# Gate and up projections of an FFN by Strassen's seven block products, with x and the inner chunks passing through DRAM

## The chip, the cores and the metric

The kernel runs on one core of one Trainium2 chip. The metric is device time in microseconds, the median of the runs. The core's engines are TensorE (PE, with PEld for its weight loads), VectorE (DVE), ScalarE (ACT), GpSimd (POOL) and SyncE (SP), which here issues all DMAs. Each takes its instructions in the order in which the program was laid out, and waits on semaphores for the others.

## The reference

One step of a decoder trunk with two layers, on 1024 prompt tokens and 8 sample tokens (T = 1032), model width 1024, all in float32:

```
x = x + short_conv(rmsnorm(x))            # layer 0: h @ w_in (1024 x 3072), a 3-tap convolution, @ w_out
x = x + swiglu(rmsnorm(x), w_gu[0], w_down[0])
k, v = rmsnorm(x) @ w_kv                  # one shared K/V, rotary on k
x = x + window_attention(rmsnorm(x) @ w_q, k, v) @ w_o      # layer 1: 16 heads, window 128, sinks
x = x + swiglu(rmsnorm(x), w_gu[1], w_down[1])
y = rmsnorm(x)

def swiglu(h, w_gu, w_down):
    g, u = split(h @ w_gu, 2)             # w_gu 1024 x 5632: 2816 columns of gate, 2816 of up
    return (silu(g) * u) @ w_down         # w_down 2816 x 1024
```

Outputs are y for both groups and the new convolution and K/V state.

## The kernel before, in words

Everything is kept transposed: the width lies in the 128 partitions, in NC = 8 chunks, and the tokens in the free dimension. x, Hh and Hl are tiles of 128 x 8 x 1032 that stay in SBUF. Tokens go in three tiles TT of 384, 384 and 264.

A product is made exact to float32 from operands split in a high and a low part (fp32r). `split` (L131) makes the high part on ACT and the low one, source minus high, on DVE; `load_w` (L79) fetches a weight unit of 1024 columns (512 KB) and splits it likewise, its subtraction on DVE, or on POOL where `lo=G`. `mm3` (L117) issues, for each row chunk, three matmuls on L122 to L124: high x high, high x low, low x high, all into one PSUM bank.

`ffn` (L346): for each of NJ = 22 column chunks j two units of weights are loaded (gate, up). For each token tile a gate group of 8 x 3 matmuls is made, multiplied by 1/rms (DVE) and put through Silu (ACT), an up group likewise, and their product split into a chunk of hidden operands fhh, fhl, which stays in SBUF. After 5, 5, 5, 3 and 4 chunks a round of the down projection (`down_round`, L220) takes the chunks gathered so far and adds into x, a bank at a time (`x_add`, L218, DVE). In the last round x is finished token tile by token tile: its squares are summed (ACT and POOL, L143 and L147), `prep` (L206) writes the next operands Hh and Hl, x times the norm's gain, and `stats` (L190) computes 1/rms. `stats` consists of `rms_tokens` (L158: matmuls against ones and eleven small DVE operations, L168 to L175, then three on L178) and `spread` (L183: a matmul), each traced a number of matmul groups later by `later` and `tick`.

Ahead of the first FFN stands the convolution, which ends in a second round of w_out (four hidden chunks) with `after_tile`. Ahead of the second FFN stands the attention: `attend` (L464) works off 32 blocks of 128 queries and one group of the samples, and fills PE's waits between them in small steps with the value rows and with `out_projection` (L658), which for a token tile loads w_o's eight units (low parts on POOL), multiplies, and adds to x. A tile's projection starts as the blocks of its tokens are done (`ends`), and what is left of the last one runs after them.

The order of instructions on each engine isn't that of the text. A planner goes through the program at compile time and takes, engine by engine, what is ready by its own reckoning, earlier lines first; buffers (wraw three, wh and wl four each, eight PSUM banks) hold it back. The order of DMAs on SP is planned in the same way.

Of the kernel before, what the change touches and what calls it, by code (L numbers as in the profile page):

```python
# [16 lines left out]
P = 128  # L17
# [29 lines left out]
def trunk_kernel(ctx, tc, A):  # L47
# [7 lines left out]

    x = const.tile([P, NC, T], F32, name="x")
# [22 lines left out]
    def load_w(src, n, lo=V, rows=None, raw=None, parts=1):  # L79
        """A weight unit as exact high and low parts; rows scales it by a norm's gain."""  # L80
# [18 lines left out]
    def mm_tile():  # L99
        return pools[-1].tile([P, 512], F32, name="mm")  # L100
# [48 lines left out]
    def token_blocks(ti):  # L149
        """(first token to sum, first column, columns) of a tile's blocks."""  # L150
        w = TT[ti][1] - TT[ti][0]
# [6 lines left out]
    def rms_tokens(acc, ti):  # L158
        """1/rms of a tile's tokens, with the tokens in the partitions."""
        at = token_blocks(ti)  # L160
# [4 lines left out]
        st = nt.tile([P, 2, 4], F32, name="nst", bufs=1)  # L165
        v, z = st[:, 0, :n], st[:, 1, :n]
        y = inv_tok[:, ti, :n]
# [15 lines left out]
    def spread(dg, ti):  # L183
        """The diagonals summed into every partition."""
        w = TT[ti][1] - TT[ti][0]
        ib = mm_tile()
        PE.matmul(ib[:, :w], ones, dg[:, :w], start=True, stop=True)
        return ib[:, :w]

    def stats(acc, ti, first, second, then=None):  # L190
        """inv of a tile, its two steps traced after as many matmul groups."""
        a, b = TT[ti]

        def one():
            dg = rms_tokens(acc, ti)

            def two():
                S.activation(inv[:, a:b], spread(dg, ti), AF.Copy)
# [7 lines left out]
    def prep(k, a, b, gi):  # L206
        """Operands of one chunk: x times the gain, still without 1/rms."""
# [12 lines left out]
    def down_round(hid, w_dram, nk, gi=None, after_tile=None):  # L220
        """x += W^T hid for nk chunks of hid; with after_tile, token tile by token tile,
        with the next phase's operands (gain gi) made as x is done."""
# [23 lines left out]
        for ti, (a, b) in enumerate(TT):  # L246
            acc = new_acc()
            for m in range(NC):
                part(units[m // per], m, a, b)
                sq_acc(acc, m, a, b)  # L250
                if gi != "final":
# [3 lines left out]
    def conv_mixer():  # L255
        with tc.tile_pool(name="cv", bufs=2) as cv:
# [9 lines left out]
            def gate(cv, i, ti, pcxb, ub, hh, hl):  # L266
                """One tile of the convolution's input, itself, and its gate."""
# [36 lines left out]
            for i in range(NC):  # L304
# [31 lines left out]
                if i == r1 - 1:  # L336
                    after = None
# [603 lines left out]
```

## Time and profile before

| | |
|---|---|
| median of 3 runs | 2292.16 us (2289.47 to 2292.61) |
| span of the profiled execution | 2287.1 us (its page gives no time beside the span) |
| PE busy | 2243.5 us, 98%, 14010 matmuls |
| DVE, ACT, POOL busy | 1028.1, 572.4, 325.0 us |
| DMA | 151.04 MB, mean 66 GB/s |

The span runs from the first to the last instruction. A busy share is the time in which an engine has an instruction at work; matmuls overlap one another, so that PE's busy time is not the sum of their durations. The two FFNs take about 1500 of the 2287 us.

### The profile page before, as it was taken

The page shows a single profiled execution, that of the slowest core. Times are in us where ns is not written, and L with a number is a line of the kernel's source. Part 1 is how long each engine was busy: PE and PEld are TensorE (multiplying, and loading weights), DVE is VectorE, ACT ScalarE, POOL GpSimd, SP SyncE. Part 2 cuts the span into 40 slices and gives each one's busy share as a digit, 9 for nine tenths or more (in the row PEclk, how much of TensorE's full clock was granted, in tenths as well). Part 3 has the DMA queues.
Part 4 walks back from the last instruction along what each step waited for, and adds up shares of the span by engine and source line. Part 5 has one row for each costly group of instructions (what it writes and reads, how often), then busy time and mean ns, then how long its engine had stood idle before and what let it go on. Part 6 is the DMA issues. An engine that isn't in the chain of part 4 may idle for free.

```text
span 2287.1 us, 33543 instructions
## 1 busy us (share of the span) xinstructions
PE 2243.5 (98%) x14010; PEld 2176.4 (95%) x14010; DVE 1028.1 (45%) x1834; ACT 572.4 (25%) x1119; POOL 325.0 (14%) x415
## 2 busy tenths in 40 slices
PE   8999999999999999999999999999999999999997
PEld 7999999999999999999899857889999999999997
DVE  7443447333333333343675465563333333333345
ACT  5110114221211211212332465542112111111122
POOL 4210114000000000000353444630000000000004
PEclk9999999999999999999999999999999999999999
DMA  5111111112112112111054554431111121111102
GB/s 189 50 56 37 56 49 45 34 35 71 34 41 65 35 40 62 40 56 47 25 174 141 152 135 121 130 93 46 39 56 46 39 61 41 46 53 51 47 29 75
DMA packets 87831, 151.04 MB, mean 66 GB/s; under 512 B 9920, under 2 KB 58576, under 8 KB 87520
## 3 DMA queue, kind: packets, MB, share of 16 engines
q1 hardware_dynamic: 87680, 148.90, 22.0%
q8 instruction: 110, 1.80, 0.3%
q14 instruction: 41, 0.34, 0.0%
HBM read 133.75 MB, written 17.23 MB: 66 GB/s over the span
## 4 chain that ended last, share of the span: by engine, by line
PE 90%; DVE 5%; ACT 2%; DMA 1%; issue 1%; POOL 1%; SPq 0%; DVEq 0%; ACTq 0%; POOLq 0%
PE mm L122 28%; PE mm L124 28%; PE mm L123 28%; PE po L569 2%; PE sc L535 1%; PE pt L555 1%; DVE Hl L133 1%; DVE x L218 1%; DMA x<-xT 1%; DVE Hl L213 1%; ACT sq L143 1%; POOL acc L147 0%; ACT Hh L212 0%; DVE inv_tok L175 0%; DVE wl L94 0%
## 5 line engine op out<-in xcount | busy, mean ns | idle before, releaser
L122 PE MATMUL mm<-Hh,wh 128*128 128x384 f32 (+1 forms) x3120 | 1003.2, 322 | 7.0 <-ACT wh L93 5.4
L123 PE MATMUL mm<-Hl,wh 128*128 128x384 f32 (+1 forms) x3120 | 1000.5, 321 | 3.5 <-DVE Hl L213 3.5
L124 PE MATMUL mm<-Hh,wl 128*128 128x384 f32 (+1 forms) x3120 | 999.2, 320 | 0.4 <-DVE wl L94 0.4
L122 PEld LDWEIGHTS mm<-Hh,wh 128*128 128x128 f32 x3120 | 588.2, 189 | 10.8 <-ACT wh L93 5.4
L123 PEld LDWEIGHTS mm<-Hl,wh 128*128 128x128 f32 x3120 | 588.3, 189 | 9.0 <-DVE Hl L213 7.4
L124 PEld LDWEIGHTS mm<-Hh,wl 128*128 128x128 f32 x3120 | 587.8, 188 | 1.8 <-DVE wl L94 1.0
L93 ACT ACTIVATE wh<-wraw 128x1024 fp32r<-128x1024 f32 (+3 forms) x222 | 216.0, 974 | 573.2 <-PE mm L123 568.5
L124 PE MATMUL mm<-fhh,wl 128*128 128x384 f32 (+1 forms) x1056 | 339.7, 322 | 0.0
L122 PE MATMUL mm<-fhh,wh 128*128 128x384 f32 (+1 forms) x1056 | 339.6, 322 | 0.0
L123 PE MATMUL mm<-fhl,wh 128*128 128x384 f32 (+1 forms) x1056 | 337.7, 320 | 0.0
L218 DVE TENSOR_TENSOR x<-mm,x 128x384 f32<-128x384 f32 (+1 forms) x312 | 159.7, 513 | 295.9 <-PE mm L124 295.5
L94 DVE TENSOR_TENSOR wl<-wraw,wh 128x1024 fp32r<-128x1024 f32 (+3 forms) x198 | 222.0, 1122 | 51.9 <-ACT wh L93 51.0
L367 DVE TENSOR_TENSOR fh<-mm,sg 128x384 f32<-128x384 f32 x132 | 68.1, 516 | 371.9 <-PE mm L124 371.9
L147 POOL TENSOR_TENSOR acc<-acc,sq 128x384 f32<-128x384 f32 (+1 forms) x105 | 111.3, 1060 | 810.2 <-ACT sq L143 806.5
L123 PEld LDWEIGHTS mm<-fhl,wh 128*128 128x128 f32 x1056 | 199.8, 189 | 0.4
L122 PEld LDWEIGHTS mm<-fhh,wh 128*128 128x128 f32 x1056 | 199.5, 189 | 0.4
L124 PEld LDWEIGHTS mm<-fhh,wl 128*128 128x128 f32 x1056 | 199.6, 189 | 0.0
L132 ACT ACTIVATE fhh<-fh 128x384 fp32r<-128x384 f32 x132 | 64.9, 492 | 378.9 <-DVE fh L368 377.1
L362 DVE TENSOR_TENSOR sg<-mm,inv 128x384 f32<-128x384 f32 x132 | 68.1, 516 | 179.2 <-PE mm L124 179.2
L363 ACT ACTIVATE sg<-sg 128x384 f32<-128x384 f32 x132 | 64.4, 488 | 285.0 <-DVE sg L362 285.0
L88 POOL TENSOR_TENSOR wraw<-wraw,sm 128x1024 f32<-128x1024 f32 x12 | 24.4, 2034 | 708.8 <-DMA wraw<-w_k 701.7
L133 DVE TENSOR_TENSOR fhl<-fh,fhh 128x384 fp32r<-128x384 f32 x132 | 67.9, 514 | 50.9 <-ACT fhh L132 50.9
(109 smaller groups left out, 1582.3 us busy)
## 6 DMA issues: line engine op xcount, KB each, us to landing
wraw<-w_gu SPq DMA_DIRECT2D x88, 512.0 KB, 3.6
q<-qd SPq DMA_DIRECT2D x128, 128.0 KB, 2.9
wraw<-w_down SPq DMA_DIRECT2D x48, 320.0 KB, 2.9
wraw<-w_o SPq DMA_DIRECT2D x24, 512.0 KB, 4.0
wraw<-w_in SPq DMA_DIRECT2D x23, 512.0 KB, 3.6
qd<-stg SPq DMA_DIRECT2D x8, 768.0 KB, 3.6
wraw<-w_out SPq DMA_DIRECT2D x8, 512.0 KB, 3.7
wraw<-w_down SPq DMA_DIRECT2D x8, 512.0 KB, 3.7
```

The lines of the kernel that those rows point to most:

```text
L93: S.activation(wh[:, c], raw[:, c], AF.Copy)
L94: lo.tensor_tensor(wl[:, c], raw[:, c], wh[:, c].bitcast(F32), op=ALU.subtract)
L122: PE.matmul(out, wh[:, c], xh, start=i == 0, stop=False)
L123: PE.matmul(out, wh[:, c], xl, start=False, stop=False)
L124: PE.matmul(out, wl[:, c], xh, start=False, stop=i == n - 1)
L132: S.activation(hi, src, AF.Copy)
L133: eng.tensor_tensor(lo, src, hi.bitcast(F32), op=ALU.subtract)
L147: G.tensor_tensor(acc[:, :w], acc[:, :w], sq[:, :w], op=ALU.add)
L218: V.tensor_tensor(x[:, m, a:b], ps, x[:, m, a:b], op=ALU.add)
L362: V.tensor_tensor(sg[:, :w], pg[:, :w], inv[:, a:b], op=ALU.mult)
L363: S.activation(sg[:, :w], sg[:, :w], AF.Silu)
L367: V.tensor_tensor(h[:, :w], pu[:, :w], sg[:, :w], op=ALU.mult)
```

## The change

Gate and up are no longer computed chunk by chunk but as a 2 x 2 block product: the width in two halves (row chunks 0 to 3 and 4 to 7), the tokens in two halves of 516 (each in two tiles of 258, FT), the output columns in pairs of chunks m and m + 11. Of the eight products of blocks seven remain, by the form of Strassen's method with 15 additions. A unit n is one such pair, of the gate (n even) or the up projection (n odd), 22 units a layer. Four additions are made on the weights (POOL, in `pair_units`), four on x (`ffn_operands`, DVE and POOL, in place), and seven on the results, of which those into one bank are made by PE, which goes on adding into it after ACT has copied its state out.

The operands are now x times gain and 1/rms, so that the factor 1/rms is no longer applied to the results. x itself is written to DRAM (xd) before it is scaled and read back before the down projection; its place in SBUF holds Strassen's differences, then temporaries of the gate and up units. The hidden chunks go to DRAM (hd) and come back, in the order HID, into Hh and Hl, four chunks at a time, for a down projection that now follows all units, in rounds of 4, 4, 4, 4, 2 and 4. The second w_out round and out_projection go by the four tiles FT; the last out_projection is left over and run inside `ffn`.

```diff
+TH = T // 2
+TS = TH // 2
+FT = [(i * TS, (i + 1) * TS) for i in range(4)]
+NP = NJ // 2
+HID = [c for m in range(NP) for c in (m, m + NP)]
-FFN_ROUNDS = [(0, 5), (5, 10), (10, 15), (15, 18), (18, 22)]
+FFN_ROUNDS = [(0, 4), (4, 8), (8, 12), (12, 16), (16, 18), (18, 22)]
...
+    xd = dr.tile([P, NC, T], F32, name="xd")
+    hd = dr.tile([NJ, P, 2, T], F32, name="hd")
...
+    k0, k1 = slice(0, 4), slice(4, 8)
+    def extra_splits(s):
+        a0, b0 = FT[s]
+        a1, b1 = FT[2 + s]
+        for e, src in enumerate((x[:, k1, a1:b1], x[:, k0, a1:b1], x[:, k1, a0:b0])):
+            split(extra["h"][:, e, :, a0:b0], extra["l"][:, e, :, a0:b0], src)
+
+    def ffn_operands(ti):
+        s = ti % 2
+        a0, b0 = FT[s]
+        a1, b1 = FT[2 + s]
+        if ti < 2:
+            for k in (k0, k1):
+                split(Hh[:, k, a0:b0], Hl[:, k, a0:b0], x[:, k, a0:b0])
+            return
+        b11, b12, b21, b22 = (x[:, k, c] for k in (k0, k1) for c in (slice(a0, b0), slice(a1, b1)))
+        split(Hh[:, k1, a1:b1], Hl[:, k1, a1:b1], b22)
+        V.tensor_tensor(b11, b12, b11, op=ALU.subtract)
+        split(Hh[:, k0, a1:b1], Hl[:, k0, a1:b1], b11)
+        G.tensor_tensor(b12, b22, b12, op=ALU.subtract)
+        V.tensor_tensor(b22, b22, b11, op=ALU.subtract)
+        G.tensor_tensor(b21, b21, b22, op=ALU.subtract)
+        if extra:
+            extra_splits(s)
+        else:
+            owed.append(s)
+
+    def ffn_tile(acc, ti, gi, first, second):
+        a, b = FT[ti]
+        Q.dma_start(xd[:, :, a:b], x[:, :, a:b])
+        def one():
+            dg = rms_tokens(acc, b - a, None)
+            def two():
+                iv = spread(dg, b - a)
+                for k in range(NC):
+                    V.scalar_tensor_tensor(
+                        x[:, k, a:b], x[:, k, a:b], gain(gi, k), iv, op0=ALU.mult, op1=ALU.mult
+                    )
+                ffn_operands(ti)
+            later(second - first, two)
+        later(first, one)
...
-        for ti, (a, b) in enumerate(TT):
+        for ti in (0, 2, 1, 3) if tiles is FT else range(len(tiles)):
+            a, b = tiles[ti]
...
+                        tiles = FT
+                        after = lambda acc, ti: ffn_tile(acc, ti, 1, 2, 5)
...
+    def pair_units(w_dram, own):
+        def load(n):
+            w = w_dram[:, n * 2048 : (n + 1) * 2048]
+            r1, r2 = fetch(w[:, 0:1024], 1024), fetch(w[:, 1024:2048], 1024)
...
+            G.tensor_tensor(s1, a21, a22, op=ALU.add)
+            parts(a11)
+            G.tensor_tensor(a21, a11, a21, op=ALU.subtract)
+            parts(s1)
+            G.tensor_tensor(a11, s1, a11, op=ALU.subtract)
+            parts(a11)
+            G.tensor_tensor(s4, a12, a11, op=ALU.subtract)
+            parts(s4)
+            parts(a21)
+            parts(a12)
+            parts(a22)
+            return dict(zip((1, 5, 6, 3, 7, 2, 4), out))
...
+        def group(ps, w, p, s, first):
+            wh, wl = w[p]
+            for k in range(4):
+                xh, xl = operand(p, k, s)
+                c = slice(k * P, (k + 1) * P)
+                for i, (lhs, rhs) in enumerate(((wh, xh), (wh, xl), (wl, xh))):
+                    PE.matmul(
+                        ps[:, s, :TS], lhs[:, c], rhs, start=first and k == 0 and i == 0,
+                        stop=k == 3 and i == 2, skip_group_check=not first,
+                    )
+            tick()
+
+        def finish(m, q, s):
+            S.activation(hi[q][:, s].bitcast(F32R), hv[q][:, s], AF.Copy)
+            V.tensor_tensor(
+                hv[q][:, s].bitcast(F32R), hv[q][:, s], hi[q][:, s], op=ALU.subtract
+            )
+            if s.stop == 2:
...
+                Q.dma_start(
+                    hd[2 * m + (q > 20), :, :, c],
+                    x[:, k, :].rearrange("p (h c) -> p h c", h=2),
+                )
...
+        def up_step(p, banks, s, m):
+            X, Y, Z = (b[:, s, :TS] for b in banks)
+            if p == 1:
+                S.activation(p1[:, s], X, AF.Copy)
+            elif p == 5:
+                S.activation(p5[:, s], Y, AF.Copy)
+            elif p == 6:
+                S.activation(u2[:, s], X, AF.Copy)
+            elif p == 3:
+                V.tensor_tensor(hv[12][:, s], Y, u2[:, s], op=ALU.add)
+                V.tensor_tensor(hv[12][:, s], hv[12][:, s], sg[12][:, s], op=ALU.mult)
+                finish(m, 12, s)
+            elif p == 7:
+                S.activation(u3[:, s], X, AF.Copy)
+                G.tensor_tensor(hv[22][:, s], u3[:, s], p5[:, s], op=ALU.add)
+                G.tensor_tensor(hv[22][:, s], hv[22][:, s], sg[22][:, s], op=ALU.mult)
+                finish(m, 22, s)
+            elif p == 2:
+                V.tensor_tensor(hv[11][:, s], Z, p1[:, s], op=ALU.add)
+                V.tensor_tensor(hv[11][:, s], hv[11][:, s], sg[11][:, s], op=ALU.mult)
+                finish(m, 11, s)
+            else:
+                V.tensor_tensor(hv[21][:, s], X, sg[21][:, s], op=ALU.mult)
+                finish(m, 21, s)
+
+        bank = {1: 0, 6: 0, 7: 0, 4: 0, 5: 1, 3: 1, 2: 2}
+        for n in range(2 * NP):
+            m, step = n // 2, up_step if n % 2 else gate_step
+            w = load(n)
+            banks = [pools[-1][0].tile([P, 2, 512], F32, name="mm2") for _ in range(3)]
+            for subs in ((0,), (1,)) if n == 0 else ((0, 1),):
+                for p in (1, 2, 5, 3, 6, 7, 4) if n == 0 else (1, 5, 6, 3, 7, 2, 4):
+                    for s in subs:
+                        group(banks[bank[p]], w, p, s, p in (1, 2, 5))
...
+    def ffn(layer, gi, after, lead=None):
...
+            for n in "hl":
+                extra[n] = ff.tile([P, 3, 4, TH], F32R, name=f"ex{n}")
+            while owed:
+                extra_splits(owed.pop(0))
...
+            if lead is not None:
+                lead()
+            gate_up(layer, ff)
...
+        for k in range(NC):
+            Q.dma_start(x[:, k], xd[:, k])
...
+            for r, (r0, r1) in enumerate(FFN_ROUNDS):
+                last = r == len(FFN_ROUNDS) - 1
+                hid = []
+                for j in range(r0, r1):
+                    if last:
+                        h = fd.tile([P, T], F32R, name=f"hh{j - r0}")
+                        l = fd.tile([P, T], F32R, name=f"hl{j - r0}")
+                    else:
+                        k = 4 * (r % 2) + j - r0
+                        h, l = Hh[:, k], Hl[:, k]
+                    Q.dma_start(h.bitcast(F32), hd[j, :, 0])
+                    Q.dma_start(l.bitcast(F32), hd[j, :, 1])
+                    hid.append((h, l))
+                down_round(hid, A[f"w_down{layer}_{r}"], r1 - r0, gi, after if last else None)
...
+        work = [Block(g, i) for i in range(SEQ // W) for g in range(NKV)]
+        work.insert(26, Samples())
+        ends = [12, 20, 29, len(work)]
```

`gate_step` does for the gate what `up_step` does for the up projection: four copies and four Silu on ACT, two additions on DVE, one on POOL. In the first w_out tiles' order (0, 2, 1, 3) tiles 0 and 2 belong to the first half product of unit 0, tiles 1 and 3 to the second. `hi` and `hv` lie in x's chunks 0 to 3, the gate's results in chunks 4 and 5, weight sums in chunks 6 and 7. For products 1 and 5 the operands are Hh's and Hl's chunks 0 to 3, for 2 and 3 chunks 4 to 7, for 6, 7 and 4 the extra splits.

## Rows read from the trace of the kernel before

**Rows 1.** Page: busy us by engine; granted clock, tenths in 40 slices.

```profile
PE 2243.5 (98%) x14010; PEld 2176.4 (95%) x14010; DVE 1028.1 (45%) x1834; ACT 572.4 (25%) x1119; POOL 325.0 (14%) x415
...
PEclk9999999999999999999999999999999999999999
```

**Rows 2.** Page, the chain that ended last: share by engine and line.

```profile
PE 90%; DVE 5%; ACT 2%; DMA 1%; issue 1%; POOL 1%; SPq 0%; DVEq 0%; ACTq 0%; POOLq 0%
PE mm L122 28%; PE mm L124 28%; PE mm L123 28%; PE po L569 2%; PE sc L535 1%; PE pt L555 1%; DVE Hl L133 1%; DVE x L218 1%; DMA x<-xT 1%; DVE Hl L213 1%; ACT sq L143 1%; POOL acc L147 0%; ACT Hh L212 0%; DVE inv_tok L175 0%; DVE wl L94 0%
```

**Rows 3.** Windows: stretch, length, busy us PE PEld DVE ACT POOL, clock, DMA.

```profile
341.00:390.00 49.00, 45.64 (x290) 44.63 (x288) 36.22 (x75) 24.14 (x48) 19.30 (x19) 1.00 0.12 36
390.00:1080.00 690.00, 689.97 (x4379) 689.64 (x4380) 260.08 (x441) 130.77 (x206) 4.22 (x4) 1.00 0.17 48
...
1266.00:1480.00 214.00, 207.74 (x1130) 154.94 (x1129) 126.87 (x230) 123.07 (x379) 108.08 (x198) 0.98 0.51 138
1480.00:1525.00 45.00, 40.70 (x277) 36.83 (x276) 31.09 (x49) 24.91 (x41) 25.89 (x17) 1.00 0.40 117
```

**Rows 4.** Timeline, PE: start, busy us, line, operation; stretches of 48, 96, 33.

```profile
646.46 0.28 PE L122 MATMUL mm<-Hh,wh 128*128 128x264 f32 x1
...
652.27 0.34 PE L122 MATMUL mm<-Hh,wh 128*128 128x384 f32 x1
...
669.09 0.28 PE L122 MATMUL mm<-Hh,wh 128*128 128x264 f32 x1
...
1268.07 0.28 PE L478 MATMUL mm<-wl,Hh 128*128 128x256 f32 x1
...
1271.99 0.28 PE L478 MATMUL mm<-wl,Hh 128*128 128x256 f32 x1
```

**Rows 5.** Lines by form: shapes, count | busy us, mean ns | idle before.

```profile
L94 DVE TENSOR_TENSOR wl<-wraw,wh 128x1024 fp32r<-128x1024 f32 x138 | 171.4, 1242 | 42.1 <-ACT wh L93 41.2 <-POOL acc L147 0.6
...
L218 DVE TENSOR_TENSOR x<-mm,x 128x384 f32<-128x384 f32 x208 | 115.4, 555 | 210.3 <-PE mm L124 209.9
...
L94 POOL TENSOR_TENSOR wl<-wraw,wh 128x1024 fp32r<-128x1024 f32 x24 | 57.8, 2413 | 17.8 <-ACT wh L93 17.6
...
L218 DVE TENSOR_TENSOR x<-mm,x 128x264 f32<-128x264 f32 x104 | 44.4, 430 | 85.6 <-PE mm L124 85.5
...
L147 POOL TENSOR_TENSOR acc<-acc,sq 128x264 f32<-128x264 f32 x35 | 36.0, 1030 | 33.6 <-ACT sq L143 32.7
...
L557 DVE TENSOR_TENSOR pc<-pt,cst 128x512 f32<-128x512 f32 x32 | 22.0, 687 | 13.9 <-PE pt L555 13.9
...
L544 ACT ACTIVATE comb<-sc 128x512 f32<-128x512 f32 x32 | 19.1, 596 | 17.8 <-PE sc L535 16.9 <-POOL comb L499 0.6
...
L784 DVE SCALAR_TENSOR_TENSOR x<-x,sm,mm 128x264 f32<-128x264 f32 x6 | 2.5, 481 | 1.8 <-ACT inv L773 1.8
```

**Rows 6.** Timeline, ACT, in the first FFN.

```profile
604.18 1.06 ACT L93 ACTIVATE wh<-wraw 128x1024 fp32r<-128x1024 f32 x1 [1.01 <-PE mm L123]
605.14 0.41 ACT L363 ACTIVATE sg<-sg 128x264 f32<-128x264 f32 x1
```

**Rows 7.** Timeline, DVE and POOL, 1497 to 1507 us.

```profile
1499.97 2.31 DVE L173 TENSOR_TENSOR nst<-inv_tok 128x3 f32<-128x3 f32 x1
...
1505.35 0.16 DVE L173 TENSOR_TENSOR nst<-inv_tok 128x3 f32<-128x3 f32 x1
...
1506.53 0.68 DVE L178 TENSOR_SCALAR dg<-cst,inv_tok 128x128 f32<-128x128 f32 x3
...
1497.53 4.74 POOL L94 TENSOR_TENSOR wl<-wraw,wh 128x1024 fp32r<-128x1024 f32 x2
```

**Rows 8.** Windows at 10 us; DMA issues, us to landing; timeline of SP.

```profile
10.00:20.00 10.00, 8.00 (x38) 6.42 (x38) 10.00 (x10) 7.46 (x15) 6.97 (x6) 1.00 1.06 381
...
qd<-stg SPq DMA_DIRECT2D x4, 528.0 KB, 4.0
...
19.37 0.63 SPq L792 DMA_DIRECT2D o_ks<-cache_k  x1
```

More of the change, by code (lines that the diff above doesn't have):

```diff
@@ L250, in down_round @@
                 sq_acc(acc, m, a, b)
-                if gi != "final":
+                if gi not in ("ffn", "final"):
                     prep(m, a, b, gi)
@@ new lines, in out_projection, with attention @@
+    def out_projection(ti):
+        a, b = FT[ti]
+        w = b - a
+        acc = new_acc()
+        xs = h_chunks(a, b)
+        for m in range(NC):
+            u = load_w(A["w_o"][:, m * 1024 : (m + 1) * 1024], 1024, lo=G)
+            ps = mm_tile()
+            for part in (range(0, 4), range(4, 8)):
+                mm3(ps[:, :w], *u, 0, xs, part)
+                yield
+            x_add(ps[:, :w], m, a, b)
+            sq_acc(acc, m, a, b)
+        ffn_tile(acc, ti, 4, 2, 4)
+    def attention(psum):
@@ L722, in attend @@
                 ti += 1
-        for _ in fill:
-            pass
+        return fill
     def start():
@@ new lines, in final, with one, two, scale @@
+    def final(acc, ti):
+        a, b = TT[ti]
+        last = b == T
+        def one():
+            dg = rms_tokens(acc, b - a, inv_tok[:, ti])
+            if last:
+                while pending:
+                    pending.pop(0)[1]()
+            later(0 if last else 2 + ti, partial(two, dg))
+        def two(dg):
+            iv = spread(dg, b - a)
+            S.activation(inv[:, a:b], iv, AF.Copy)
+            for n in range(4):
+                later(0 if last else n + ti, partial(scale, iv, 2 * n))
+        def scale(iv, k0):
+            for k in (k0, k0 + 1):
+                y = x[:, k, a:b]
+                if k in ((1, 4, 7), (), (4, 5))[ti]:
+                    G.tensor_tensor(y, y, inv[:, a:b], op=ALU.mult)
+                    S.activation(y, y, AF.Copy, scale=gain(5, k))
+                else:
+                    V.scalar_tensor_tensor(
+                        y, y, gain(5, k), iv, op0=ALU.mult, op1=ALU.mult
+                    )
+            Q.dma_start(A["o_y"][:, k0 : k0 + 2, a:b], x[:, k0 : k0 + 2, a:b])
+        later(0 if last else 2, one)
@@ new lines, in finish_tile @@
+    def finish_tile(rest):
+        for _ in rest:
+            pass
+    with tc.tile_pool(name="ps1", bufs=8, space=bass.MemoryType.PSUM) as psp:
+        pools.append((psp, False))
+        conv_mixer()
+        pools.pop()
+    psum = ffn(0, None, lambda acc, ti: stats(acc, ti, 2, 4 if ti == 2 else 8))
+    rest = attention(psum)
+    psum = ffn(1, "final", final, partial(finish_tile, rest))
+    psum.close()
+    Q.dma_start(A["o_ks"], A["cache_k"])
+    Q.dma_start(A["o_vs"], A["cache_v"])
@@ L800, in _units, with _quarters @@
         w[(k0 + k) * P : (k0 + k + 1) * P, c] for c in cols for k in range(nk)
+    ]
+def _quarters(w, pairs):
+    return [
+        w[(4 * h + k) * P : (4 * h + k + 1) * P, _chunk_cols(m)]
+        for pair in pairs for h in range(2) for m in pair for k in range(4)
     ]
```

250 lines of the change are left out of this document (127 added, 123 removed).

## The prediction

> **What bounds the kernel now.** Read in this order. First the page's busy shares [rows 1]: TensorE (PE) is busy 98% of the span, DVE 45%, ACT 25%, POOL 14%, and the reader should see nines in the granted clock from end to end. Then the chain that ended last [rows 2]: 90% of it is PE, 28% on each of the three lines of mm3. Then the stretches [rows 3]: in the first FFN (the second is alike) PE is busy 689.97 of 690 us, while DVE has 260. Nothing there waits, so a matmul taken out of an FFN is time taken out. PE stands still only where phases meet: 3.4 us of 341 to 390 (conv to FFN) and 4.3 us of 1480 to 1525 (attention to FFN). What a matmul costs isn't its busy time (they overlap) but the distance between starts [rows 4]: 48 starts with 264 columns take 652.27 - 646.46 = 5.81 us, 121.0 ns each; the next 96 with 384 columns take 16.82 us, 175.2 ns each; 33 with 256 columns take 3.92 us, 118.8 ns each.
>
> **Gate and up, what goes and what comes.** Before, a layer has 44 column chunks x 8 row chunks x 3 matmuls = 1056 per token tile; over two layers 4224 wide ones and 2112 of 264 columns: 4224 x 0.1752 + 2112 x 0.1210 = 995.6 us. After, a layer has 22 units x 7 products x 4 row chunks x 3 x 2 half tiles = 3696 of 258 columns, 7392 in all: fewer columns by 1/8, but more instructions. No row has 258 columns. From below 258/384 of 175.2 ns = 117.7 ns, from above a line through the rows with 256 and 264 columns, 119.4. I take 119 ns, since the 256 row is nearest: 879.6 us (870.1 to 882.6). Taken away: 116.0 us (113.0 to 125.5).
>
> Tiles of 258 also come into the second w_out round (4 x 96 x 0.119 = 45.7 us for 45.3) and into w_o (+0.9): together +1.3. The down projection keeps its columns. Its sixth round adds 24 x_add a layer, beside PE: a round of two chunks has 8 x 6 x (2 x 0.1752 + 0.1210) = 22.6 us of PE and 16 x 0.555 + 8 x 0.430 = 12.3 us of DVE adds [rows 5].
>
> **Inside the loop of units.** One unit is 168 x 0.119 = 20.0 us of PE, a product 2.86 us. The helpers, by [rows 5], with 512 columns on ACT at 0.60, DVE at 0.69, POOL at 1.3 (between 1.03 at 264 columns and 2.41 at 1024): seven weight splits and eight evacuations on ACT, 7 x 0.6 + 8 x 0.6 = 9.0 us; on DVE in an up unit seven weight subtractions and nine operations on the results, 16 x 0.69 = 11.0 us; on POOL four weight sums and, in an up unit, two operations more, 7.8 us. All fit in 20. Products 1, 6, 7, 4 grow in one bank, and each must be read by ACT (0.6 us) before the next is added; another product of 2.86 us lies between, so the reading is covered 4 times over. The same cover stands for the last product, which the next unit's second one waits for. Weight parts are made while the unit before runs: the order on an engine isn't the order of the text, since [rows 6] ACT makes the next chunk's wh at 604.18, ahead of the Silu of the present one. I take 3 us for both layers (0 to 25).
>
> A rule speaks against this loop. In the trace, DVE's L173 on three elements takes 2.31 us while a POOL subtraction of 2.4 us runs, and 0.16 us without one; it ends as POOL's ends [rows 7]. The Trainium skill (SBUF — State Buffer, "SBUF: two separate sides") says the same: a DVE operation with two SBUF inputs and a POOL operation share a pair of ports as an exclusive lock, and the later one blocks. In an up unit two-input work of DVE is 13 x 0.69 = 9.0 us, so by the rule the pair is held 9.0 + 7.8 = 16.8 of 20.0 us: tight, but not the bound, and this term stays.
>
> **Conv to FFN, the dear place.** Count from the start of the second w_out round; a tile is 96 x 0.119 = 11.4 us, the round ends at 45.7. All of the following falls on DVE [rows 5, 7], and SBUF-only work of 1032 columns is taken at 1.25 from the 1024 row. Statistics 11 operations 0.2 apart and 0.68: 2.9. Scaling x, eight at 0.48: 3.9. Operands: tiles 0 and 1 two subtractions, 2.5; tiles 2 and 3 four operations, 5.0, and three extra splits, 3.75. From 14.3 us, when tile 0's sum is there, until product 5 of the second half can start: tile 0 9.3, tile 2 11.8, tile 1 9.3, tile 3 as far as its difference's low part 10.6, 22 x_add 9.5, unit 0's weights 4.8, the first half's extra splits 3.75: 59 us, so 73.3 at the earliest. PE wants that product after 45.7 + 9 half products of 1.43 = 58.6. A gap of 15 us. POOL holds 16 us of additions, 9.6 of differences and 5 of weight sums in that time; if a tenth of it blocks DVE, 3 us more (0 to 19, its share beside two-input work). Less the 3.4 us that PE loses there now [rows 3]: +15 (8 to 31).
>
> **Attention to FFN.** The last w_o tile (22.8 us) runs after the blocks, so tile 2's operands have cover. Tile 3's chain of 10.6 can't start before 22.8 + 2.9 (two groups of unit 0), so it ends at 36.3, where PE wants product 5 at 22.8 + 9 x 1.43 = 35.7. Tile 2's 15.5, x_add's 3.4 and the weights' 4.8 lie before it on DVE, 27 us from about 3 us on. POOL has w_o's low parts at 2.4 each, four differences and the weight sums; half of these last 14.6 us held against DVE makes 7. Gap about 8, less 4.3 of now: +4 (0 to 25). In attention itself eight more w_o units cost POOL 19 us of 214, where it is busy 108 [rows 3]: hidden but for +2 (0 to 10).
>
> **Gate and up to down.** x and four hidden chunks come back from DRAM. The chunks are 8 loads of 528 KB, 4.3 MB; at the 381 GB/s that 10 to 20 us shows 11.3 us, and 4.0 us for the first [rows 8]. Hh's first half is free after product 5 of the last unit, 5 x 2.86 = 14.3 us before the end, so these loads are covered. x's first chunk waits for the stores of product 2 (0.69 x 3 + 0.6 + 4.0 = 6.7 us after it) and queues behind the second round's eight loads: it lands some 11 us after the end. x_add is then late, but eight banks hold eight tiles, 15 us of PE. That holds if SP lets a ready load pass a waiting one. It does so where the planner saw it so: o_ks, last in the text, is issued at 19.37 [rows 8]. I take 2.5 us at each of two places (0 to 22). Over the down rounds 22 x 1.06 MB + 11.5 MB in 249 us is 139 GB/s, far below 381.
>
> **The sum.** 2287.1 - 116.0 + 1.3 + 3 + 15 + 4 + 2 + 5 = 2201.4 us of span. The page's execution gives its span alone; the median of the runs, 2292.16, lies 5.1 above it. Forecast 2206.5 us.
>
> **Rivals.**
> - The meeting points cost no more than now, because the planner lets other work into DVE's waits: 2287.1 - 114.7 + 5.1 + some 4 = 2182 us. For it: DVE is at 74% in 341 to 390 [rows 3] and PE lost only 3.4 us. Against: the sum of 59 us on one engine. 20%.
> - Loads in the wrong order and POOL's holds in full. If x's loads stand ahead of the chunks on SP, the first group of each down phase waits about 6.7 + 11.3 + 4.0 = 22 us, twice, where I have 5; with POOL's holds in full at conv to FFN 16 more: 2206.5 + 39 + 16 = 2261.5 us, half of it 2234. For it: x's loads come first in the text. 12%.
> - Slower than before: late reading in the bank that four products share. ACT and DVE take work in order, and DVE can hang behind POOL. If every reading there ends later than 2.86 us after its product, PE waits at 4 x 44 = 176 places. It decides from (2292.2 - 2206.5)/176 = 0.49 us of lateness on; at 1 us the time is 2206.5 + 176 = 2382.5. For it: DVE's waits for POOL [rows 7], and that ACT's copies stand behind copies that wait for DVE. Against: four-fold cover and ACT at half load. That the change doesn't save matmul time because a weight load bounds 258 columns is excluded by the 118.8 ns at 256 columns. 6%.
>
> **Chances.** Forecast (2192 to 2230) 60%, the rivals 20, 12 and 6; 2% within 0.2% of now, which is about what a measurement of this kernel can tell from no change. So faster 0.92, same 0.02, slower 0.06. The range reaches from the first rival to the dear case, 2178 to 2255, and leaves out some 15%.
>
> **What would show it.** Starts of 258-column matmuls 118 to 119.5 ns apart, 168 of them in about 20 us; no PE wait inside units. In the round before the first FFN, DVE busy without a break and PE idle some 15 us ahead of the second half of unit 0. At both starts of the down phase, PE idle below 5 us and the chunks' loads issued before those of x's first chunks. It would be wrong if units last more than 20.7 us (a wait a product), or if the meeting points cost over 70 us together.

## The result, and the profile after

The changed kernel takes 2251.99 us (median of 4 runs, 2251.54 to 2253.41) against 2291.85 for the kernel before beside it: ratio 0.9828 [0.9814, 0.9842]. The forecast was 2206.5. The gain is there, 39.9 us, but less than half of the 85.7 forecast. The profiled execution has a span of 2251.6 us, 35.5 less than before.

The page's busy shares and clock, which answer to [rows 1], and its chain by engine and line [rows 2]:

```profile
PE 2166.4 (96%) x15370; PEld 2093.3 (93%) x15370; DVE 1127.8 (50%) x1896; ACT 743.5 (33%) x1421; POOL 697.6 (31%) x689
...
PEclk9999999999999999999999999898999999999998
...
PE 87%; DVE 6%; POOL 2%; ACT 2%; issue 2%; DMA 1%; SPq 0%; DVEq 0%; POOLq 0%; ACTq 0%
PE mm L500 38%; PE mm L135 14%; PE mm L136 14%; PE mm L137 14%; PE po L838 2%; DVE Hl L146 1%; PE sc L804 1%; POOL acc L160 1%; PE pt L824 1%; DMA x<-xT 1%; DVE x L229 1%; ACT Hh L145 1%; PE mm L176 0%; POOL wl L103 0%; ACT sq L156 0%
```

POOL's work has doubled, the clock row has lost its unbroken nines, and PE has given 3% of the chain to the helpers. Where that is, the windows say (columns as in [rows 3]):

```profile
341.00:390.00 49.00, 39.55 (x313) 39.01 (x312) 34.53 (x78) 15.40 (x31) 27.57 (x28) 0.92 0.23 66
390.00:440.00 50.00, 38.63 (x251) 36.04 (x251) 42.71 (x75) 24.76 (x43) 19.14 (x15) 0.87 0.15 44
440.00:860.00 420.00, 420.00 (x3499) 420.00 (x3498) 183.18 (x257) 177.82 (x310) 151.99 (x112) 1.00 0.36 117
1400.00:1470.00 70.00, 62.83 (x357) 47.67 (x357) 42.00 (x82) 35.48 (x92) 43.63 (x50) 0.87 0.51 142
1470.00:1520.00 50.00, 39.20 (x304) 36.31 (x302) 30.44 (x48) 20.10 (x29) 35.81 (x21) 0.91 0.37 105
1520.00:1570.00 50.00, 40.72 (x274) 38.77 (x275) 36.12 (x52) 22.92 (x42) 25.16 (x17) 0.84 0.23 74
1565.00:1985.00 420.00, 417.14 (x3473) 416.94 (x3472) 187.76 (x261) 177.68 (x309) 151.56 (x112) 1.00 0.36 117
```

The reader is to see two things. Between 440 and 860 us the loop of units keeps PE busy 420.00 of 420 us, with every helper below half load. Around it PE is idle 21 of 99 us at conv to FFN and 27 of 170 at attention to FFN, where before it was idle 3.4 and 4.3 (in 49 and 45 us). The waits of PE in these two stretches (engine and line that waited, what for: us in total, times, longest), 340 to 440 first:

```profile
PE mm L176 <- POOL acc L160: 13.8, 3, 8.1
PE mm L500 <- DVE Hl L146: 3.0, 1, 3.0
```

and 1480 to 1600:

```profile
PE mm L500 <- DVE wl L146: 12.0, 1, 12.0
PE mm L500 <- ACT wh L145: 3.0, 1, 3.0
PE mm L500 <- DVE Hl L146: 2.6, 1, 2.6
```

For a ledger, read the starts of PE's matmuls: from the start of the second w_out round to the first scores of the attention ("first place": conv to FFN, first FFN, rotary) and from there to the last matmul ("second place": attention, its end, second FFN). Before they last 940.9 and 999.6 us, after 914.4 and 992.2. With 258-column matmuls at the 120.1 ns that the loop shows, matmuls alone would make them 887.8 and 947.4. So the first place costs 26.6 us more than before and the second 44.8, beside what the matmuls save. Together with 105.3 us saved on matmuls and 1.6 ahead of the first place: -105.3 + 26.6 + 44.8 - 1.6 = -35.5, the change of the span.

### The profile page after: what moved, and what is told of

It is laid out like the page before. It is cut to its first block, busy times and chain, and to the rows that moved or that the text cites. A ratio compares the mean times of both kernels' runs of the same rounds, so it can differ in the third digit from the quotient of the medians.

```text
span 2251.6 us, 37629 instructions
## 1 busy us (share of the span) xinstructions
PE 2166.4 (96%) x15370; PEld 2093.3 (93%) x15370; DVE 1127.8 (50%) x1896; ACT 743.5 (33%) x1421; POOL 697.6 (31%) x689
## 4 chain that ended last, share of the span: by engine, by line
PE 87%; DVE 6%; POOL 2%; ACT 2%; issue 2%; DMA 1%; SPq 0%; DVEq 0%; POOLq 0%; ACTq 0%
PE mm L500 38%; PE mm L135 14%; PE mm L136 14%; PE mm L137 14%; PE po L838 2%; DVE Hl L146 1%; PE sc L804 1%; POOL acc L160 1%; PE pt L824 1%; DMA x<-xT 1%; DVE x L229 1%; ACT Hh L145 1%; PE mm L176 0%; POOL wl L103 0%; ACT sq L156 0%
## 5 line engine op out<-in xcount | busy, mean ns | idle before, releaser
L135 PE MATMUL mm<-Hh,wh 128*128 128x384 f32 (+2 forms) x1936 | 614.7, 318 | 8.3 <-ACT wh L102 5.4
L136 PE MATMUL mm<-Hl,wh 128*128 128x384 f32 (+2 forms) x1936 | 613.4, 317 | 2.8 <-DVE Hl L224 2.8
L137 PE MATMUL mm<-Hh,wl 128*128 128x384 f32 (+2 forms) x1936 | 611.5, 316 | 2.7 <-POOL wl L103 2.6
L500 PE MATMUL mm<-Hh,wl 128*128 128x258 f32 x1408 | 400.6, 285 | 12.0 <-DVE wl L146 12.0
L500 PE MATMUL mm<-Hl,wh 128*128 128x258 f32 x1408 | 401.5, 285 | 5.6 <-DVE Hl L146 5.6
L500 PE MATMUL mm<-Hh,wh 128*128 128x258 f32 x1408 | 402.8, 286 | 4.0 <-ACT wh L145 3.0
L500 PE MATMUL mm<-exh,wh 128*128 128x258 f32 x1056 | 299.0, 283 | 2.3 <-ACT u L532 2.0
L500 PE MATMUL mm<-exl,wh 128*128 128x258 f32 x1056 | 298.8, 283 | 1.2 <-DVE exl L146 1.2
L500 PE MATMUL mm<-exh,wl 128*128 128x258 f32 x1056 | 299.4, 284 | 0.0
L500 PEld LDWEIGHTS mm<-Hh,wl 128*128 128x128 f32 x1408 | 269.2, 191 | 12.4 <-DVE wl L146 12.4
L500 PEld LDWEIGHTS mm<-exh,wh 128*128 128x128 f32 x1056 | 200.2, 190 | 3.6 <-ACT u L532 2.8
```

Of the source, the lines that this page charges most:

```text
L135: PE.matmul(out, wh[:, c], xh, start=i == 0, stop=False)
L136: PE.matmul(out, wh[:, c], xl, start=False, stop=False)
L137: PE.matmul(out, wl[:, c], xh, start=False, stop=i == n - 1)
L500: PE.matmul(ps[:, s, :TS], lhs[:, c], rhs, start=first and k == 0 and i == 0, stop=k == 3 and i == 2, skip_group_check=not first,)
```

## The experiments

Each is the changed kernel with the edit shown, unless it says otherwise. "Places" are the added costs by that ledger, from each profiled execution. Where nothing was edited in it, the first moves by some 2 us (26.4 to 28.3 in e2, e12, e15 and e16), but the second by 8: e3, whose edit lies in the first place, has 36.6 there. Differences of that size aren't read; where the 8 us come from is shown under "The clock". The changed kernel was not run again beside the edits, so two runs are taken as different where the intervals of their ratios are apart.

| run | us, median | ratio to before | places |
|---|---|---|---|
| changed kernel | 2251.99 | 0.9828 [0.9814, 0.9842] | 26.6, 44.8 |
| e1_ops_dve | 2242.62 | 0.9774 [0.9759, 0.9790] | 23.1, 41.1 |
| e2_wo_dve | 2252.32 | 0.9823 [0.9806, 0.9839] | 26.5, 42.9 |
| e3_stats_late | 2251.21 | 0.9821 [0.9799, 0.9843] | 29.4, 36.6 |
| e4_tiles258 | 2308.60 | 1.0066 [1.0053, 1.0079] | |
| e6_defer | 2246.45 | 0.9798 [0.9777, 0.9819] | 23.2, 37.8 |
| e7_no_extras | 2265.94 | 0.9886 [0.9870, 0.9901] | 37.0, 45.9 |
| e8_bare | 2242.77 | 0.9784 [0.9771, 0.9797] | 23.8, 35.5 |
| e10_defer_both | 2238.42 | 0.9758 [0.9743, 0.9774] | 21.6, 34.2 |
| e11_bare_k1 | 2218.31 | 0.9678 [0.9665, 0.9692] | 9.4, 28.1 |
| e12_keep_warm | 2249.53 | 0.9814 [0.9799, 0.9828] | 28.3, 39.0 |
| e13_best | 2233.56 | 0.9750 [0.9736, 0.9765] | 21.4, 31.1 |
| e14_defer_ops | 2242.79 | 0.9788 [0.9775, 0.9801] | 23.3, 34.8 |
| e15_late | 2247.69 | 0.9812 [0.9798, 0.9825] | 26.6, 39.0 |
| e16_wo_all | 2250.12 | 0.9821 [0.9808, 0.9835] | 26.4, 40.8 |
| e17_best2 | 2238.53 | 0.9771 [0.9754, 0.9788] | 21.8, 30.7 |
| e18_best3 | 2233.91 | 0.9750 [0.9737, 0.9764] | 20.6, 31.2 |

The first theories, on what holds PE up where phases meet (the "meeting points"): A, POOL is late there and the other queues stand behind it; B, DVE has too much to do; C, PE's own order puts a waiting instruction ahead of ready ones.

**The price of the matmul.** The kernel before, with gate and up in four tiles of 258 tokens and no Strassen:

```diff
-                for a, b in TT:
+                for a, b in [(i * 258, (i + 1) * 258) for i in range(4)]:
```

> The kernel before with gate and up groups in four token tiles of 258 in place of 384, 384 and 264, no block products: the price of the narrower matmul by itself. At the 119 ns of the forecast two layers gain 2 x 1056 x (4 x 119 - 471.4 ns) = 9.7 us, 2302 us; at the 120.1 ns that lie between starts in the changed kernel 19 us, 2311 us. If narrow tiles bring waits of their own (evacuations, weights), more than 2316.

It took 16.6 us more than the kernel before. 8448 such matmuls replace 995.6 us, so one costs (995.6 + 16.6)/8448 = 119.8 ns. In the changed kernel itself, two starts, the second 51 matmuls after the first (timeline of PE, columns as in [rows 4]):

```profile
599.77 0.28 PE L500 MATMUL mm<-exh,wh 128*128 128x258 f32 x1
...
605.89 0.28 PE L500 MATMUL mm<-Hh,wh 128*128 128x258 f32 x1
```

That is 120.0 ns each.

**POOL's differences moved to DVE** (e1):

```diff
-        G.tensor_tensor(b12, b22, b12, op=ALU.subtract)
+        V.tensor_tensor(b12, b22, b12, op=ALU.subtract)
...
-        G.tensor_tensor(b21, b21, b22, op=ALU.subtract)
+        V.tensor_tensor(b21, b21, b22, op=ALU.subtract)
```

> The changed kernel with the two subtractions of ffn_operands that were on POOL (1032 columns, 2.4 us each) made on DVE. Theory A, POOL is late where phases meet and PE waits in order behind it: the 8.1 us for which PE waits for POOL's sum of squares in the second w_out round go to under 3, time 2240 to 2246 us. Theory B, the amount of DVE work at the meeting points is what lasts: DVE gets 2.5 us more a tile, time 2254 to 2262. Theory C, PE's own order is at fault, the statistics' matmul standing ahead of groups that don't need it: the wait stays above 6 us, time 2250 to 2254.

9.4 us came back, as A expected; PE's longest wait for the sums fell from 8.1 to 5.0 us, not under 3. The timeline of the changed kernel at conv to FFN, DVE and then POOL, shows why taking work onto the busier engine helps:

```profile
376.17 5.02 DVE L146 TENSOR_TENSOR Hl<-x,Hh 128x1032 fp32r<-128x1032 f32 x2
381.11 1.22 DVE L257 TENSOR_TENSOR x<-x 128x1032 f32<-128x1032 f32 x1
382.25 1.41 DVE L229 TENSOR_TENSOR x<-mm,x 128x258 f32<-128x258 f32 x4
...
376.00 2.42 POOL L256 TENSOR_TENSOR x<-x 128x1032 f32<-128x1032 f32 x1 [3.07 <-DVE x L254]
378.38 1.72 POOL L160 TENSOR_TENSOR acc<-acc,sq 128x258 f32<-128x258 f32 x1
382.41 2.37 POOL L258 TENSOR_TENSOR x<-x 128x1032 f32<-128x1032 f32 x1 [2.31 <-DVE x L257]
384.74 2.67 POOL L160 TENSOR_TENSOR acc<-acc,sq 128x258 f32<-128x258 f32 x3
```

and the same splits in e1, with the difference now on DVE:

```profile
375.86 2.37 DVE L146 TENSOR_TENSOR Hl<-x,Hh 128x1032 fp32r<-128x1032 f32 x2
378.14 1.23 DVE L256 TENSOR_TENSOR x<-x 128x1032 f32<-128x1032 f32 x1
```

Beside POOL the two splits take 5.02 us, alone 2.37, and the difference itself is 1.23 us instead of 2.42. The Trainium skill (SBUF — State Buffer, "SBUF: two separate sides") lets such a pair of operations hold the shared ports one after the other; the trace agrees, 2.37 + 2.42 being close to 5.02. What POOL did "in parallel" here was paid by DVE in full. And the w_out round itself hangs on it: four x_adds stand behind the operands until 382.25, the sums they feed on POOL behind L258 until 384.74, and PE, which has the sums' matmul next, waits its 8.1 us.

**The low parts of w_o's last tile on DVE** (e2):

```diff
-u = load_w(A["w_o"][...], 1024, lo=G)
+u = load_w(A["w_o"][...], 1024, lo=V if ti == 3 else G)
```

> The changed kernel with the low parts of w_o's eight units for the last token tile on DVE in place of POOL. Theory A: POOL is free for unit 0's weight sums, on which ACT waits 5.6 us with the operands' high parts behind it, so PE's wait of 12 us before the second FFN's first product falls under 4, time 2239 to 2246 us. Theory B: DVE gets 8 x 1.24 = 10 us more in front of the same operands, time 2254 to 2264. Theory C: no change, 2250 to 2254.

A expected a gain, and there was none. First the changed kernel at its 12 us wait, timelines of ACT, DVE, POOL and PE:

```profile
1500.30 0.63 ACT L145 ACTIVATE wh<-wraw 128x512 fp32r<-128x512 f32 x1 [0.76 <-PE mm L136]
1506.51 0.63 ACT L145 ACTIVATE wh<-wraw 128x512 fp32r<-128x512 f32 x1 [5.57 <-POOL wraw L442]
1507.05 2.01 ACT L145 ACTIVATE Hh<-x 128x1032 fp32r<-128x1032 f32 x2
...
1508.14 4.85 DVE L146 TENSOR_TENSOR Hl<-x,Hh 128x1032 fp32r<-128x1032 f32 x2 [5.54 <-ACT Hh L145]
...
1515.54 4.33 DVE L146 TENSOR_TENSOR exl<-x,exh 128x1032 fp32r<-128x1032 f32 x2
...
1520.45 1.82 DVE L146 TENSOR_TENSOR wl<-wraw,wh 128x512 fp32r<-128x512 f32 x2
...
1501.11 3.41 POOL L103 TENSOR_TENSOR wl<-wraw,wh 128x1024 fp32r<-128x1024 f32 x1
...
1505.18 1.29 POOL L442 TENSOR_TENSOR wraw<-wraw 128x512 f32<-128x512 f32 x1
...
1521.18 0.58 PE L500 MATMUL mm<-Hh,wl 128*128 128x258 f32 x1 [11.98 <-DVE wl L146]
```

Read it backwards. PE waits for the low part of product 1's weight, whose high part was there at 1500.9. On DVE that low part stands behind tile 2's splits; these wait for ACT, whose copy of tile 2 stands behind a copy of a weight sum; the sum waits for POOL, which still makes w_o's low parts. Three queues in order make one chain. In e2 POOL's link is gone, and DVE runs without a break, operands first (timelines of DVE and PE):

```profile
1499.18 5.05 DVE L146 TENSOR_TENSOR Hl<-x,Hh 128x1032 fp32r<-128x1032 f32 x2
...
1506.78 4.33 DVE L146 TENSOR_TENSOR exl<-x,exh 128x1032 fp32r<-128x1032 f32 x2
...
1511.36 1.42 DVE L103 TENSOR_TENSOR wl<-wraw,wh 128x1024 fp32r<-128x1024 f32 x1
1512.70 1.22 DVE L146 TENSOR_TENSOR wl<-wraw,wh 128x512 fp32r<-128x512 f32 x1
...
1512.83 0.58 PE L137 MATMUL mm<-Hh,wl 128*128 128x258 f32 x1 [9.70 <-DVE wl L103]
```

PE now waits 9.7 us one step earlier, for the last low part of w_o itself (made at 1511.36), which the edit has put into DVE's queue; product 1's low part follows at 1512.70 and is not waited for. A alone falls: behind POOL's lateness lies DVE's own queue, where extra splits that only products 6, 7 and 4 read, the last of unit 0, are ahead of w_o's last weight and of the weights that product 1 reads.

**PE's order in the last w_out round** (e3):

```diff
-ffn_tile(acc, ti, 1, 2, 5)
+ffn_tile(acc, ti, 1, 5, 8)
```

> The changed kernel with the two steps of the statistics in the second w_out round traced after 5 and 8 groups in place of 2 and 5. Theory C: the statistics' matmul no longer stands in front of PE's ready groups, the 8.1 us go to under 1 and nothing else moves, time 2242 to 2246 us. Theory A: POOL's sum still comes late and the operands later, half of it is gained, 2246 to 2250. Theory B: all operands come later by up to three groups, 4 us, time 2252 to 2258.

The waits for the sums went, and one of 14.3 us for dg, the norm's last step on DVE, came in their place (waits of PE, 330 to 460 us of this run):

```profile
PE mm L198 <- DVE dg L190: 14.7, 2, 14.3
PE mm L500 <- ACT inv L525: 5.2, 2, 2.9
```

C falls: PE's order only chose which late thing it waits for.

**Order or amount?** New theories: order (work that nobody needs yet stands ahead in DVE's queue) against amount. e6 records the first half's extra splits behind unit 0's weights:

```diff
-        if extra:
+        if extra and s:
             extra_splits(s)
         else:
...
             w = load(n)
+            while owed:
+                extra_splits(owed.pop(0))
...
-            while owed:
-                extra_splits(owed.pop(0))
```

> At both meeting points the three extra splits of the first half (read only by the sixth, third and last product) are recorded behind the weights of unit 0 instead of ahead of them. Order theory (work that nobody needs yet stands in DVE's queue ahead of the low part that PE waits for): the wait of 12.0 us ahead of unit 0 of layer 1 loses the 1.22 + 4.33 us that these splits took on DVE there, and the 3.4 us gap at layer 0 shrinks; 2243 to 2247 us against 2251.99 for the changed kernel. Amount theory (DVE has that much to do before unit 0 can end, in whatever order): the wait moves to the products that read the extra operands, 2250 to 2254.

2246.45 is in the order theory's interval, but the runs spread (2239.27 to 2253.07) and the ratio's interval overlaps the changed kernel's: the time doesn't decide. The waits moved as the order theory has it, in part: PE's wait of 12.0 us shrank to 7.9, that for a weight's high part grew from 3.0 to 5.1.

e10 joins e1, e2 and e6:

> Three edits together, output whole: differences on DVE (2242.6 alone), the low parts of w_o on DVE for the last tile (2252.3 alone), extra splits behind the weights of unit 0. In the run with w_o alone the wait had moved to DVE's queue, 9.7 us behind 14.6 us of operand work. Order theory: the three add up once the queue is in order, 2230 to 2238. Amount theory: DVE now has all of it, no better than the differences alone, 2241 to 2247.

e14 is the same with w_o's low parts left on POOL:

> Differences on DVE and extra splits behind the weights of unit 0, with the low parts of w_o left on POOL. Sum of the two edits measured alone (9.4 and 5.5 us): 2237. If the low parts of w_o on DVE count for something once the queue is in order (2238.4 with all three): 2241 to 2245. If the two edits mend the same wait: 2241 to 2244 also, but then with the wait ahead of unit 0 of layer 1 no longer than in the run of the three.

2238.4 and 2242.8, with intervals that just part. So the low parts, worth nothing alone, seem to be worth some 4 us in the medians once DVE's queue is in order. e14 is no better than e1, and e10's interval overlaps e1's: deferring the splits adds nothing that these runs can tell. The mends don't add up: each uncovers the next queue.

**Leaving the operand work out.** e7 leaves out the extra splits, e8 also the block differences (products without operands of their own read Hh and Hl):

> Leaves out the extra splits altogether (12 on ACT and 12 on DVE in all); the third, sixth and seventh product read the splits that are there. Their DVE time is six of 1.2 to 2.2 us at each meeting point. Order theory: little better than deferring them, 2240 to 2246. Amount theory: all of it comes back, 16 to 20 us, 2232 to 2236.

> Leaves out the extra splits and also the four block differences of each half tile pair; the second tiles are only split. Takes 2 x (1.23 + 1.22) us of DVE and 2 x (2.4 + 2.4) us of POOL more off each meeting point, and with POOL's differences DVE's slow splits beside them (2.5 instead of 1.2 us). If the operands are what fills the meeting points: 2210 to 2225. If it is the chain from the last w_out or w_o group through sums, norm and scaling, and the seven weight splits: 2232 to 2242. The floor, with both meeting points as cheap as in the kernel before and 120.1 ns for a matmul, is about 2195.

e7 was slower than the changed kernel, which no theory had. The waits of PE from 845 to 900 us show a new stall in the down projection:

```profile
PE mm L135 <- DMA Hh<-hd: 12.5, 2, 12.2
```

And the timeline of SP's queue, e7:

```profile
854.74 0.60 SPq L617 DMA_DIRECT2D Hh<-hd  x1
...
865.56 4.99 SPq L598 DMA_DIRECT2D x<-xd  x4
870.64 0.38 SPq L617 DMA_DIRECT2D Hh<-hd  x1
```

against the changed kernel:

```profile
847.78 0.90 SPq L625 DMA_DIRECT2D Hh<-hd  x2
...
850.27 0.43 SPq L625 DMA_DIRECT2D Hh<-hd  x1
...
865.83 0.56 SPq L606 DMA_DIRECT2D x<-xd  x1
```

With the extra operands gone, a late product (7) reads Hh's first half, so the hidden chunks that go there can't be loaded early, and they fall behind x's loads. This is the loading order of the prediction's second rival, made by accident: 12.5 us at the first down start, 10.0 at the second. e8, at 2242.77 in neither of its intervals, has the same two stalls (12.6 and 7.9 us). e11 is e8 with products 6, 7 and 4 reading Hh's second half, so that the first half is free after product 5, as in the changed kernel:

> Leaves out the same work as the run without extra splits and block differences (2242.8 us), but lets the third, sixth and seventh product of a unit's order that no longer have operands of their own read the upper half of Hh and Hl, so that the lower half is read last by the first and fifth product as in the changed kernel. That earlier run had new stalls in the first round of the down projection, 12.4 and 8.2 us, which the changed kernel does not have. If they come from chunk loads that wait for the last reader of Hh and stand behind the eight loads of x in SP's queue: both go, and the time is 2222 to 2228, so that operands cost some 27 us at the meeting points. If they come from something else (the DRAM hand-over as such): 2239 to 2245.

Both stalls went, 2218.3. The operands' differences and extra splits, with what they hold up, cost 33.7 us: 17.2 at the first place and 16.7 at the second, in which PE's idle time falls by 14.8 and 13.6 us.

**The clock.** Behind its longer waits the changed kernel's PE is granted half speed for some microseconds; two windows behind the wait of 8.1 us and one behind a wait of 4.4 (columns as above):

```profile
388.50:392.30 3.80, 3.80 (x19) 3.80 (x19) 3.12 (x9) 0.42 (x1) 1.98 (x3) 0.50 0.00 0
392.50:394.30 1.80, 1.80 (x17) 1.80 (x16) 1.62 (x6) 1.16 (x3) 0.29 (x1) 1.00 0.00 0
408.30:412.70 4.40, 4.40 (x22) 4.40 (x22) 1.86 (x7) 1.67 (x2) 0.64 (x1) 0.50 0.41 119
```

At 1.2 GHz (0.50) the starts lie 0.215 us apart, at 2.4 GHz (1.00) 0.120. e12 fills layer 1's long wait with matmuls whose result is unused:

```diff
+        spare = [84] if layer else []
...
+                    if spare and i == 2:
+                        bank = mm_tile()
+                        for _ in range(spare.pop()):
+                            PE.matmul(bank[:, :TS], wh[:, c], xh, start=True, stop=True)
```

> The changed kernel with 84 more matmuls of 258 columns (10.1 us at 0.12) into a spare bank, put in PE's order just ahead of the matmul of layer 1's unit 0 that waited 12.26 us; their result is not used. Clock theory (after a wait PE runs at 1.2 GHz, starts 0.21 us apart, and this is what the stretch pays): the slow starts between 1473 and 1600 us, 7.8 us in all, go down, 2245 to 2249. Supply theory (the next groups wait for their operands anyway, so a faster PE only waits longer): 2250 to 2254. If the added matmuls are themselves granted 1.2 GHz they take 18 us and outlast the wait: 2256 to 2260.

2249.53. Between 1520 and 1570 us the clock rose from 0.84 to 0.97, but the next waits stayed (2.3 us for Hl, 1.8 for ACT), and ahead of the added matmuls PE still waited 5.9 us, for an x_add. The gain is 2.5 us and the intervals overlap: this run doesn't price the half clock.

Two kept traces do. e3's edit lies in the first place; in the attention, from the first scores to the end of the last values, it has the same matmuls as the changed kernel, but another clock (windows, changed kernel, then e3):

```profile
1251.50:1478.90 227.40, 217.86 (x1258) 159.75 (x1258) 141.15 (x263) 128.62 (x384) 119.26 (x204) 0.93 0.52 143
1255.30:1474.70 219.40, 209.78 (x1258) 154.43 (x1258) 141.14 (x263) 128.40 (x384) 119.70 (x204) 0.97 0.54 149
```

PE is idle 9.5 and 9.6 us in them and works 29.9 and 13.7 us at half clock, and the stretch differs by 8.0 us: about half of each microsecond at half clock is lost, and the waits don't take it back. Why the clock stayed low for less long in e3, behind the same waits, no run shows. Within a kernel too the time goes with the mean granted clock: e3's runs reach from 2247.43 us at 0.982 to 2259.15 at 0.976, e6's from 2239.27 at 0.984 to 2253.07 at 0.977.

With this price the ledger can be split. The windows of the first and second place, kernel before, then the changed one:

```profile
338.70:1279.60 940.90, 926.95 (x5883) 923.58 (x5881) 418.01 (x725) 212.73 (x360) 108.13 (x91) 1.00 0.20 62
1279.60:2279.10 999.50, 987.99 (x6089) 930.66 (x6090) 444.10 (x799) 289.62 (x647) 150.00 (x230) 0.99 0.24 67
...
337.10:1251.50 914.40, 883.66 (x6515) 878.53 (x6513) 463.44 (x756) 294.87 (x507) 284.54 (x224) 0.99 0.37 124
1251.50:2243.70 992.20, 954.75 (x6818) 893.16 (x6818) 498.57 (x830) 378.53 (x802) 346.36 (x371) 0.97 0.40 128
```

PE's idle time (length less busy) grew by 16.8 and 25.9 us. Its work at half clock, from the granted clock of each stretch of the trace, grew from 6.5 to 21.4 us in the first place and from 10.8 to 43.4 in the second: by the starts above some 7 and 15 us, an estimate. Of the 71.4 us some 7 are left that neither explains.

**Inside the attention.** e15 spreads the norm of w_o's tiles 0 and 1 later, e16 puts all of w_o's low parts on DVE:

```diff
-ffn_tile(acc, ti, 4, 2, 4)
+ffn_tile(acc, ti, 4, 2, 6 if ti < 2 else 4)   # e15
-u = load_w(A["w_o"][...], 1024, lo=G)
+u = load_w(A["w_o"][...], 1024, lo=V)          # e16
```

> One edit to the changed kernel: the norm of w_o's tiles 0 and 1 is spread six groups after the tile's end instead of four. PE waited 3.98 us there for dg in the middle of the attention. Wait theory: this is part of the 15 us that the attention's stretch (first scores to the end of w_o) lost more than before; 2246 to 2249 against 2251.99. Shared-limit theory (the blocks of the attention set the pace, the wait is filled by what they would have waited for): 2250 to 2254.

> One edit to the changed kernel: all low parts of w_o on DVE, 32 of 1.23 us instead of 32 of 2.4 to 3.4 us on POOL. POOL theory (three tiles of 258 instead of two of 384 ask POOL for a third more low parts while the attention's own POOL work stands beside them): PE's waits of 2.0 and 1.2 us for low parts go, DVE's small steps no longer run beside POOL, 2243 to 2248. If the waits for low parts only give way to DVE's queue, as they did for the last tile alone (2252.3): 2250 to 2255.

From the first scores to the last values the changed kernel takes 226.9 us (209.9 before); e15 takes 215.4 and e16 213.6. Not all of that is their doing: e3, with nothing edited here, takes 218.9. In e15 PE is idle 4.3 us less in this stretch, but 2.9 us more behind it; in e16 58 of the 1258 matmuls, 7 us, run behind it instead. 4.3 and 1.9 us are left in the medians, and both intervals overlap the changed kernel's.

**A better version.** e13 is e10 with e15's edit and w_o's low parts on DVE for the last two tiles; e18 has all of them there; e17 is e18 with the last w_out tiles' norm one group later (3 and 6).

> The three edits together (2238.4 us) and two more inside the attention: the low parts of w_o on DVE for the last two tiles instead of the last, and the spreading of the norm of w_o's tiles 0 and 1 six groups after the tile's end instead of four (PE waited 3.98 us there for dg, and 2.0 us for a low part from POOL). If these waits are the price that the narrower w_o tiles add inside the attention: 2231 to 2235. If the time of that stretch is set by the blocks of the attention or comes back as another wait: 2237 to 2241.

> All edits so far (2233.6 us with the low parts of w_o's last two tiles on DVE), now with all of w_o's low parts there, and the norm of the last w_out tiles one group later (3 and 6 instead of 2 and 5), so that PE reaches the sums, for which it still waits 5.3 and 1.6 us, after work that is ready. If PE's own order is part of those waits: 2225 to 2230. If the sums come late because DVE's queue is full, so that the wait moves on as it did when they were put five groups back: 2231 to 2236.

> The same without the later norm of the last w_out tiles, to tell the two edits apart: all of w_o's low parts on DVE on top of the version at 2233.6. POOL theory: 2228 to 2232. If DVE's queue takes the wait's place: 2233 to 2237.

2233.6, 2238.5, 2233.9. e13 and e18, which are alike, are the fastest with the whole computation, 18 us under the changed kernel. e10's interval overlaps theirs, so what the edits inside the attention add isn't told from nothing; and PE's own order once more gained nothing.

## Why the prediction was wrong

**The steps that failed** are two. The first is "Attention to FFN", "+4", with "In attention itself ... +2". With half of the loop's 3 and of the down starts' 5, it stood for 10 us at the second place; measured are 44.8, of which 25.9 are idle time. It counted when the last tile's operands are due at product 5 and gave the work ahead of it 27 us on DVE (its terms 15.5, 3.4 and 4.8 add up to 23.7), taking tile 2's operands as covered. But PE stopped 12.0 us at product 1, for a weight: nothing in the sum asked in which order DVE, ACT and POOL, each in order, would deliver what the first product reads. Without the operand work 13.6 us less are idle (e11), and queue order and engine choice give back 10.5 (e13); these overlap. How the rest divides between w_o's low parts, the weight splits and the sums is not settled.

The second is a term put at nothing: every wait is counted as idle time alone, and the nines of the granted clock before are taken to stay. Around the new waits PE works 14.9 and 32.6 us more at half clock, which costs some 7 and 15 us. With the operand work left out, 28.1 us of added cost remain at the second place, 12.4 of them idle; by the same price the half clock (39.7 us of work, 10.8 before) makes some 13 of the others.

**Conv to FFN, +15 (8 to 31)**: with the other halves 19, measured 26.6, inside its range. As idle time the size was nearly right, 16.8, and the half clock is about what is over. The cause was right, DVE's chain of operands; its share is 17.2 us. The place was not: half of the idle time lies inside the w_out round, where PE waits for sums whose x_add stands behind operand work on DVE, not ahead of unit 0's second half, so that the size is in part luck. POOL's holds were put at 3 us here; e1, which takes only the differences off POOL, gave back 9.4 over both places.

**Matmuls, -116.0**: 120.1 ns instead of 119, 8 us. The value lay nearer to the row with 264 columns [rows 4] than to the one taken.

**Profiled execution and median**: 5.1 us between them before, 0.4 after: the forecast gains 4.7 by that.

So the error is 34.8 (second place) + 7.6 (first place) + 9.4 (all matmuls, with w_out and w_o) - 1.6 (ahead of the first place) - 4.7 = 45.5 us. The prediction's own sign of being wrong, meeting points over 70 us together, came: 71.4.

**Right**: the loop of units, with no wait in 420 us; the readings of the shared bank, so the slow rival did not occur; SP's order, with the chunks issued at 847.4 to 850.3 ahead of x at 865.8; down starts of 0 and 2.9 us instead of 2.5 each. What that order is worth e7 shows: the rival's price of 22 us at each was 12.5 and 10.0.

## What to carry to other kernels

Where a phase begins, don't add up an engine's work against the last thing that is due: write down, for the first instruction that PE will run, the queue of each helper up to its operand, in the order in which the helpers will run it. Work that is needed late but recorded early stands in that queue, and a helper that waits for another passes the wait on. Price the waits with the clock: here, beside 42.7 us of new idle time, work at half clock cost some 22 us more. Two-input work moved from DVE to POOL is no relief while DVE works on SBUF operands too (e1).

## What the runs showed of the hardware

A 258-column matmul costs 120.0 ns start to start, nearly as much as one of 264 columns (121.0); two columns more than 256 (118.8, in another stream of the kernel before) cost 1.2 ns. The Trainium skill (TensorE: Matmul & The Clock Gate, "Back-to-back issue gap") gives N/2.4 + 2.5 ns for the isolated gap, by estimate 110.0 for 258; in this stream, which loads a weight for each matmul, the trace shows 120.0, and the measurement decides.

The half clock behind PE's waits shows in the granted clock, not in busy time: in the window from 388.50 PE is "busy" 3.80 of 3.80 us, with starts 0.215 us apart instead of 0.120. Two executions of the same stretch with the same idle time differ by 8.0 us through it (227.40 us at a mean clock of 0.93, 219.40 at 0.97).
